# Another order of the products in a feed-forward block, partial sums carried in PSUM by ScalarE, six load places and five split places

## The chip, the cores and the metric

The kernel runs on one core of a Trainium2 chip. The metric is the device time of one execution in microseconds (us). The core has five engines that take part: TensorE (PE) multiplies matrices and writes to PSUM, VectorE (DVE) and ScalarE (ACT) do elementwise work, GpSimd (POOL) does a little arithmetic and issues the accumulating transfers, SyncE (SP) issues all other transfers. Each engine runs its instructions strictly in the order in which the program gives them.

## The reference

Two layers act on x of 256 tokens by 1024 features, in float32. Each layer is a half-step feed-forward network (FFN), a mixer, and a second half-step FFN, each between two RMS norms:

```
def _swiglu(h, wg, wu, wd):
    return (jax.nn.silu(h @ wg) * (h @ wu)) @ wd
...
for l in range(DEPTH):
    f = _swiglu(_rmsnorm(h, ff1_norm_pre[l]), ff1_w_gate[l], ff1_w_up[l], ff1_w_down[l])
    h = h + 0.5 * _rmsnorm(f, ff1_norm_post[l])
    m = _hybrid_mixer(_rmsnorm(h, mix_norm_pre[l]), w_in[l], conv_w[l], conv_b[l], dt_bias[l],
                      a_log[l], d_skip[l], ssd_norm[l], pool_w[l], pool_scale[l], w_out[l])
    h = h + _rmsnorm(m, mix_norm_post[l])
    f = _swiglu(_rmsnorm(h, ff2_norm_pre[l]), ff2_w_gate[l], ff2_w_up[l], ff2_w_down[l])
    h = h + 0.5 * _rmsnorm(f, ff2_norm_post[l])
```

wg and wu are 1024 x 2816, wd is 2816 x 1024. The mixer (state-space heads, pooling, attention) is the same in both kernels. The change concerns the FFNs, of which there are four in a run, and the planner that orders everything.

## The kernel before, in words

**Weights.** Every weight matrix is cut into units of 128 partitions x 2048 float32 (1 MB). A unit is loaded into a `raw` place. Then it is *split* for the multiplication: ScalarE writes `hi`, a copy rounded to the format that TensorE multiplies, and VectorE writes `lo` = raw - hi. A product then takes hi x hi, lo x hi and hi x lo. So each unit costs ScalarE one pass, VectorE one pass and TensorE 12 matmuls of 128x512 (24 for a unit of `wd`, a *down*, which serves both token tiles). There are `RAW_BUFS` = 4 raw places and `SPLIT_BUFS` = 6 places for hi and for lo.

**A block.** Of the 2816 hidden columns of an FFN, columns 512 to 2559 are done in four blocks of 512 (`QUADS`). A block computes the gate and the up projection for both token tiles (0 and 1) by seven products in place of eight (the Strassen-Winograd scheme), on four units: g1, g2 (gate weights, upper and lower half of the features) and u1, u2 (up weights). The products, with the name that the code gives them, the left operand and the weights:

| product | left operand | weights | PSUM bank | how the weights come about |
|---|---|---|---|---|
| g1 | X11 | g1 | pa | loaded |
| T1 | S1 | g1+u1 | pc | VectorE adds u1 into g1's raw place |
| g2 | X12 | g2 | pa, added | loaded |
| u2 | S4 | u2 | pc, added | loaded |
| T2 | S2 | g1+u1+u2 | pb | a DMA issued by GpSimd adds u2 from memory onto the place of g1+u1 |
| T3 | S3 | u1+u2 | pd | a second such DMA adds u2 onto the place of u1 |
| T4 | X22 | g1+u1+u2+g2 | pd, added | VectorE adds g2 into that place |

The two accumulating DMAs can start once T1's sum has read u1 (for T3's weights) and once T1's split has read g1+u1 (for T2's weights). `h0` and `h1` are the results for token tiles 0 and 1; `w2` is a scratch tile. Between the products stand `0` and `1` (the *turns*: TensorE transposes h0 and h1 of the block before, ScalarE and VectorE split them) and `d` (one *down* of the block before: 24 matmuls into the banks `acc`). The list `ORDER` gives the sequence. Bank names in the profile: pa to pd and the turns' banks are `wk` (four places); the turned and split hidden values are `t`; the left operands X are in `xT`, the left operands S in `n`.

**The order.** The program writes its operations to a `Planner`, which sets the order of every engine before anything is emitted: `cost` gives each operation a duration, `arrange` counts latest start times back from TensorE's order (`late`; the allowance for a dependency is `gap` plus a pad), and then runs a list schedule, in which the free places of `raw`, `hi`, `lo` and `wk` count too. It emits the operations in that order (`emit`, line 354 of the kernel before: all instructions of the profile carry that line, so tiles tell them apart). The semaphores that enforce dependencies are put in afterwards, so an estimate in the planner changes only the order. In the code, `Weights` makes loads and splits, `plan_ffn.block` lists the jobs of a block, `product` issues 12 matmuls, `ffn_quad` is the block.

Of the kernel before, what the change touches and what calls it, by code (L numbers as in the profile page):

```python
# [14 lines left out]
AF = mybir.ActivationFunctionType  # L15
# [14 lines left out]
UNIT = 2048  # L30
QDT = 264
PEKEY = 0
PAD = 300.0
TMP, NBUF, ROUNDS = 14, 8, 1
RAW_BUFS = 4
PF, FINE = 2, 'g1 T1 g2'.split()
AHEAD = "".split()
ORDER = "g1 0 T1 1 g2 d T3 T2 d u2 T4".split()
SUMMED = "T3 T2".split()
SPLIT_BUFS = 6  # L40
TAIL = 4

FIRST, QUADS, PAIRS = (0, 1), (2, 4, 6, 8), (10,)
# [95 lines left out]
        return lambda *args, **kw: self.plan.add(self.engine, name, args, kw)  # L139


class Planner:


# [55 lines left out]
    def cost(self, o, views):  # L200
        width = max(v.cols for _, v in views)
        psum = any(v.tile.tag in BANKS for _, v in views)
        e, kind = o.engine, o.name
        o.kind, o.tail = kind, 0.0
        if e == "tensor":
            x = o.args[2] if kind == "matmul" else o.args[1]
            n = x.cols / 2.4
            if kind == "transpose":
                o.busy = 2 * n + 2
            elif x.dtype == F32R:  # L210
                o.busy = n + 14
            elif x.dtype == BF16:
                o.busy = n + 3
            else:
                o.busy = 4 * n + 8
                if x.rows[1] - x.rows[0] <= 64:
                    o.busy /= 2
            o.tail = 205.0
        elif e == "vector":
            o.busy = 1.042 * width + 68 if kind != "memset" else 0.5 * width  # L220
            if kind == "scalar_tensor_tensor":
                o.busy += 0.125 * width
            o.tail = 82.0
        elif e == "scalar":
            func = o.args[2]
            o.busy = 0.844 * width + (60 if psum else 92)
            o.tail = 100.0
            if any(isinstance(v, View) for v in (o.kw.get("scale"), o.kw.get("bias"))):
                o.busy += 90
            if "accum_out" in o.kw:  # L230
                o.busy, o.tail = o.busy + 95, 150.0
            o.kind = {AF.Exp: "exp", AF.Silu: "silu"}.get(func, "any")
        elif o.name == "dma_start":
            x = next(v for _, v in views)
            size = x.cols * 4 * (x.rows[1] - x.rows[0]) / 424.0
            o.kind = "dma"
            o.busy, o.tail = (880.0, size) if e == "gpsimd" else (330.0, size)
        else:
            o.busy, o.tail = 800.0, 0.0

    def gap(self, p, o, why):
        if why == "ORDER":
            return 0.0
        if p.engine == o.engine and p.kind != "dma":
            return p.busy + p.tail + LAG[p.engine, p.engine] if why == "RAW" and p.engine != "tensor" else 0.0
        return p.busy + p.tail + LAG.get((p.engine, o.engine), 55.0)

    def arrange(self, target=None):
        ops = self.ops
        post = [[] for _ in ops]  # L250
        for o in ops:
            for p, why in o.pre.items():
                post[p.n].append((o, self.gap(p, o, why) + (3500.0 + p.tail if p.kind == "dma" else PAD if p.engine != "tensor" else 0)))
        if target is None:
            at, target = 0.0, {}
            for o in ops:
# [7 lines left out]
        ready = [0.0] * len(ops)  # L264
        hand = {e: [o for o in ops if o.engine == e and not o.pre] for e in ENGINES}
        free = dict.fromkeys(ENGINES, 0.0)
        line, idle, table = 0.0, 0.0, "any"
        turn = dict.fromkeys(self.slots, 0)
        places = {k: [(0.0, i) for i in range(n)] for k, n in self.slots.items()}
        for t in self.tiles:  # L270
# [32 lines left out]
        while len(order) < len(ops):  # L303
# [13 lines left out]
                busy += 1300.0 * (table not in ("any", o.kind))  # L317
                table = o.kind
            if o.kind == "dma":
                line = max(s + (600 if e == "sync" else 1500), line) + o.tail * (1 if e == "sync" else 1.5)  # L320
                done = line + o.tail * (0 if e == "sync" else 0.5) + 1700.0
            else:
                done = s + busy + o.tail
            if e == "tensor":
# [97 lines left out]
def hybrid_trunk_kernel(ctx: ExitStack, tc: tile.TileContext, a, out: bass.AP):  # L422
# [200 lines left out]
    def plan_ffn(l, n):  # L623
# [11 lines left out]
        def block(i, src, before):  # L635
# [14 lines left out]
            for s in steps:  # L650
                if s == "d":
                    jobs.append((s, None, None, None))
                    continue
                if s == "g1":
                    k, y = "g1", None
                elif s in ("g2", "u2"):
                    k, y = s, None
                elif s == "T3":
                    k, y = "u1+u2" if "T3" in AHEAD else "u1", None
                elif s == "T1" and "T1" in AHEAD:  # L660
                    k, y = "g1+u1", None
                else:
                    k = "g1+u1" if "T1" in AHEAD else "g1"
                    y = chain[s]
                jobs.append((s, k, y if s not in SUMMED else None, y if s in SUMMED else None))
# [96 lines left out]
    def ffn_quad(i, p, left, turn, downs):  # L762


        tiles = {}
        downs = list(downs)
        for s in ORDER:
            if s in "01":
                turn(int(s))
            elif s == "d":  # L770
                if downs:
                    downs.pop(0)()
            elif s == "g1":
                pa = bank()
                product(pa, left["X11"], p[s, i], True)
                w2 = buf()
                nc.scalar.activation(w2, pa, AF.Copy)
            elif s == "T1":
                pc = bank()
                product(pc, left["S1"], p[s, i], True)  # L780
                h1 = buf()
                nc.scalar.activation(h1, pc, AF.Copy)
            elif s == "T2":
                pb = bank()
                product(pb, left["S2"], p[s, i], True)
                nc.vector.tensor_tensor(w2, pb, w2, op=ALU.add)
                nc.vector.tensor_tensor(pc, pc, w2, op=ALU.subtract)
                tiles["T2"] = 1
                if "T3" in tiles:
                    nc.vector.tensor_tensor(pd, pd, w2, op=ALU.add)  # L790
                    nc.vector.tensor_tensor(h1, h1, pd, op=ALU.subtract)
            elif s == "T3":
                pd = bank()
                product(pd, left["S3"], p[s, i], True)
                tiles["T3"] = 1
                if "T2" in tiles:
                    nc.vector.tensor_tensor(pd, pd, w2, op=ALU.add)
                    nc.vector.tensor_tensor(h1, h1, pd, op=ALU.subtract)
            elif s == "g2":
                product(pa, left["X12"], p[s, i], False)  # L800
                h0 = buf()
                nc.scalar.activation(h0, pa, AF.Silu)
            elif s == "T4":
                product(pd, left["X22"], p[s, i], False)
                nc.scalar.activation(w2, pd, AF.Silu)
                nc.vector.tensor_tensor(h1, h1, w2, op=ALU.mult)
            elif s == "u2":
                product(pc, left["S4"], p[s, i], False)
                nc.vector.tensor_tensor(h0, pc, h0, op=ALU.mult)
        assert not downs  # L810
        return [h0, h1]

# [594 lines left out]
```

## Time and profile before

| | us |
|---|---|
| median of 3 runs | 960.19 |
| lowest and highest | 953.47, 962.56 |
| the profiled execution, its own time | 959.03 |
| its span, first to last instruction | 957.2 |

| engine | busy us | share | instructions |
|---|---|---|---|
| TensorE, matmuls | 924.6 | 97% | 4666 |
| VectorE | 806.0 | 84% | 915 |
| ScalarE | 589.0 | 62% | 799 |
| GpSimd | 54.0 | 6% | 67 |

The granted TensorE clock of the execution is 0.993. The run is, in order: first FFN, mixer, second FFN of layer 0, then the same of layer 1. Busy time of TensorE in the profile is the union of its matmuls' spans, and their ends are modelled, so a stretch that is 100% busy need not be one in which it works at its full rate. Columns of the timeline views: start, time taken, engine, line, operation, output<-inputs, count, and in brackets the idle time before it and what ended that.

### The profile page before, as it was taken

To read this page: it belongs to the slowest core of one execution; us is meant where nothing else is said; L and a number is where in the kernel's file an instruction comes from. 1 tells how busy PE (TensorE), PEld (TensorE's weight loads), DVE (VectorE), ACT (ScalarE), POOL (GpSimd) and SP (SyncE) were. 2 spreads that over 40 slices of the span, in tenths; PEclk is the share of its full clock that TensorE was granted. 3 is DMA by queue.
4 is the path that set the end of the run, shared out by engine and by line. 5 is a ranking of instruction groups with operands and counts; after the bars stand their busy time and mean duration, and the time that the engine had idled before them with its cause. 6 is when DMAs were issued, how large, how long until landed. Compare 5 with 4: busy or idle time off the path is not lost.

```text
span 957.2 us, 12144 instructions
## 1 busy us (share of the span) xinstructions
PE 924.6 (97%) x4666; PEld 768.8 (80%) x4666; DVE 806.0 (84%) x915; ACT 589.0 (62%) x799; POOL 54.0 (6%) x67
## 2 busy tenths in 40 slices
PE   8999999999999999998999999899999999999997
PEld 5878777989988887777988887688998888887796
DVE  6898898889879889888699898886898799889862
ACT  7656656678647746655577565656694576646641
POOL 0000000010002000000020000000000010000000
PEclk9999999999999999999999999999999999999999
DMA  8968877955434887887568787884743277797821
GB/s 340 284 224 261 246 228 265 346 201 196 157 126 127 231 257 243 250 255 290 193 173 294 194 256 271 226 315 157 253 151 132 91 194 264 220 274 240 276 89 45
DMA packets 30878, 211.46 MB, mean 221 GB/s; under 512 B 3426, under 2 KB 3682, under 8 KB 6244
## 3 DMA queue, kind: packets, MB, share of 16 engines
q1 hardware_dynamic: 26212, 177.13, 49.4%
q0 software_dynamic: 4608, 33.56, 18.4%
q8 instruction: 37, 0.61, 0.2%
q14 instruction: 21, 0.17, 0.1%
HBM read 209.62 MB, written 1.05 MB: 220 GB/s over the span
## 4 chain that ended last, share of the span: by engine, by line
PE 32%; DVE 15%; DMA 11%; ACT 5%; issue 5%; DVEq 0%; POOLq 0%; POOL 0%; ACTq 0%
PE wk L354 22%; DMA raw<-in_ff_q 11%; PE acc L354 10%; DVE lo L354 10%; ACT hi L354 5%; DVE raw L354 4%; DVE t L354 1%; DMA raw<-in_ff_d 1%; ACT t L354 0%; DVE h L354 0%; DVEq L1403 0%; DVE n L354 0%; POOLq L1403 0%; POOL s L354 0%; ACTq L354 0%
## 5 line engine op out<-in xcount | busy, mean ns | idle before, releaser
L354 DVE TENSOR_TENSOR lo<-raw,hi 128x2048 fp32r<-128x2048 f32 (+3 forms) x300 | 482.6, 1632 | 78.5 <-ACT hi L354 76.9
L354 ACT ACTIVATE hi<-raw 128x2048 fp32r<-128x2048 f32 (+3 forms) x300 | 406.5, 1386 | 226.6 <-DVE raw L354 91.1
L354 PE MATMUL acc<-hi,t 128*128 128x512 f32 x832 | 217.3, 392 | 1.2 <-DVE t L354 1.0
L354 PE MATMUL wk<-hi,xT 128*128 128x512 f32 (+1 forms) x832 | 213.1, 387 | 5.2 <-DVE t L354 2.9
L354 PEld LDWEIGHTS acc<-hi,t 128*128 128x128 f32 x832 | 154.8, 188 | 35.0 <-DVE t L354 3.2
L354 PEld LDWEIGHTS wk<-hi,xT 128*128 128x128 f32 x832 | 149.6, 188 | 39.1 <-issue 5.6
L354 PE MATMUL wk<-hi,n 128*128 128x512 f32 x512 | 142.7, 406 | 14.1 <-DVE t L354 7.1
L354 PEld LDWEIGHTS wk<-hi,n 128*128 128x128 f32 x512 | 96.4, 193 | 39.6 <-issue 11.9
L354 PE MATMUL acc<-lo,t 128*128 128x512 f32 x416 | 114.2, 390 | 0.0
L354 ACT ACTIVATE t<-wk 128x512 f32<-128x512 f32 (+2 forms) x194 | 85.5, 480 | 41.6 <-PE wk L354 32.3
L354 PE MATMUL wk<-lo,xT 128*128 128x512 f32 (+1 forms) x416 | 108.3, 383 | 1.5 <-DVE lo L354 1.5
L354 PEld LDWEIGHTS acc<-lo,t 128*128 128x128 f32 x416 | 78.1, 188 | 16.5
L354 PEld LDWEIGHTS wk<-lo,xT 128*128 128x128 f32 x416 | 76.2, 188 | 18.0 <-DVE lo L354 2.7
L354 DVE TENSOR_TENSOR t<-wk,t 128x256 fp32r<-128x256 f32 (+1 forms) x140 | 71.0, 517 | 14.5 <-ACT t L354 14.3
L354 PE MATMUL wk<-xT,hi 128*128 128x256 f32 x576 | 77.1, 284 | 0.0
L354 PE MATMUL wk<-lo,n 128*128 128x512 f32 x256 | 72.7, 407 | 1.9 <-DVE lo L354 1.9
L354 PEld LDWEIGHTS wk<-xT,hi 128*128 128x128 f32 x576 | 72.6, 191 | 1.6 <-issue 0.7
L354 DVE TENSOR_TENSOR raw<-raw,raw 128x2048 f32<-128x2048 f32 (+1 forms) x36 | 73.5, 2049 | 0.3
L354 PEld LDWEIGHTS wk<-lo,n 128*128 128x128 f32 x256 | 49.0, 193 | 15.1 <-DVE lo L354 3.2
L354 POOL TENSOR_TENSOR s<-s,halfexp 128x1 f32<-128x1 f32 x28 | 25.3, 902 | 479.3 <-ACT s L354 337.6
L354 POOL DMA_DIRECT2D raw<-in_ff_q x32 | 28.1, 879 | 418.8 <-DVE t L354 268.5
L354 DVE TENSOR_TENSOR n<-acc,gains 128x512 f32<-128x512 f32 x24 | 16.5, 690 | 34.9 <-ACT n L354 34.9
(91 smaller groups left out, 562.1 us busy)
## 6 DMA issues: line engine op xcount, KB each, us to landing
raw<-in_ff_q SPq DMA_DIRECT2D x64, 1024.0 KB, 5.4
raw<-in_ff_d SPq DMA_DIRECT2D x44, 1024.0 KB, 6.5
raw<-in_ff_q POOLq DMA_DIRECT2D x32, 1024.0 KB, 9.0
raw<-in_ff_f SPq DMA_DIRECT2D x16, 1024.0 KB, 4.8
raw<-in_w_in SPq DMA_DIRECT2D x10, 1024.0 KB, 4.8
raw<-in_w_kvz SPq DMA_DIRECT2D x8, 1024.0 KB, 5.3
raw<-in_w_out SPq DMA_DIRECT2D x8, 1024.0 KB, 4.8
gains<-in_gains SPq DMA_DIRECT2D x11, 512.0 KB, 6.5
```

The source lines that it names most:

```text
L354: getattr(getattr(nc, o.engine), o.name)(*map(put, o.args), **{k: put(v) for k, v in o.kw.items()})
```

## The change

1. `ORDER`, the sequence of a block, goes from `g1 0 T1 1 g2 d T3 T2 d u2 T4` to `g1 0 T1 g2 1 d u2 T2 d T3 T4`.
2. The partial sums of the Winograd scheme are carried otherwise. Before, T2 and T3 go into empty banks and VectorE adds the earlier sums afterwards (`w2 = pb + w2`, `pc -= w2`, `pd += w2`, `h1 -= pd`). Now ScalarE copies g1's product from bank pa to bank pb, T2 is multiplied onto it, ScalarE copies pb to bank pd (and to w2), and T3 and T4 are multiplied onto that. VectorE keeps `pc -= w2`, `h1 -= pd`, `h0 = pc*h0` and `h1 *= w2`. Per block VectorE loses two operations of 128x512 and ScalarE gains two.
3. `RAW_BUFS` 4 to 6, `SPLIT_BUFS` 6 to 5; the memory taken is the same (4 + 2x6 and 6 + 2x5 tiles of one size).
4. The planner's idea of a transfer: a new class `Loads` keeps the two DMA queues apart and lets them share when they overlap; sizes are divided by 355 (SP) and 210 (GpSimd) in place of 424, and the allowances before a transfer's user change from 3500 + tail to 2500 (SP) or `MORE` = 6000 (GpSimd).

No matmul, no load and no split is added or taken away; GpSimd's sequence of operations is the same.

```diff
-PAD = 300.0
+PAD, MORE, LATE = 300.0, 6000.0, 2000.0
-RAW_BUFS = 4
+RAW_BUFS = 6
-ORDER = "g1 0 T1 1 g2 d T3 T2 d u2 T4".split()
+ORDER = "g1 0 T1 g2 1 d u2 T2 d T3 T4".split()
-SPLIT_BUFS = 6
+SPLIT_BUFS = 5
...
+class Loads:
+    def __init__(self):
+        self.end, self.spans, self.share = [0.0, 0.0], [[], []], (0.32, 0.68)
+
+    def add(self, which, t, work):
+        t = start = max(t, self.end[which])
+        part = self.share[which]
+        for a, b in self.spans[1 - which]:
+            if b <= t:
+                continue
+            alone = max(a - t, 0.0)
+            if work <= alone:
+                break
+            work -= alone
+            t += alone
+            if work <= (b - t) * part:
+                t, work = t + work / part, 0.0
+                break
+            work -= (b - t) * part
+            t = b
+        t += work
...
-            size = x.cols * 4 * (x.rows[1] - x.rows[0]) / 424.0
+            size = x.cols * 4 * (x.rows[1] - x.rows[0])
-            o.busy, o.tail = (880.0, size) if e == "gpsimd" else (330.0, size)
+            o.busy, o.tail = (880.0, size / 210.0) if e == "gpsimd" else (330.0, size / 355.0)
...
+        if p.kind == "dma":
+            return p.tail + (MORE if p.engine == "gpsimd" else 2500.0)
...
-                line = max(s + (600 if e == "sync" else 1500), line) + o.tail * (1 if e == "sync" else 1.5)
-                done = line + o.tail * (0 if e == "sync" else 0.5) + 1700.0
+                done = loads.add(1, s + 2800, o.tail) + LATE if e == "gpsimd" else loads.add(0, s + 1500, o.tail) + 1500
...
             elif s == "g1":
                 pa = bank()
                 product(pa, left["X11"], p[s, i], True)
-                w2 = buf()
-                nc.scalar.activation(w2, pa, AF.Copy)
...
             elif s == "T2":
-                pb = bank()
-                product(pb, left["S2"], p[s, i], True)
-                nc.vector.tensor_tensor(w2, pb, w2, op=ALU.add)
-                nc.vector.tensor_tensor(pc, pc, w2, op=ALU.subtract)
-                if "T3" in tiles:
-                    nc.vector.tensor_tensor(pd, pd, w2, op=ALU.add)
-                    nc.vector.tensor_tensor(h1, h1, pd, op=ALU.subtract)
+                product(pb, left["S2"], p[s, i], False)
+                pd = bank()
+                nc.scalar.activation(pd, pb, AF.Copy)
+                w2 = buf()
+                nc.scalar.activation(w2, pb, AF.Copy)
+                nc.vector.tensor_tensor(pc, pc, w2, op=ALU.subtract)
+                if done:
+                    nc.vector.tensor_tensor(h0, pc, h0, op=ALU.mult)
             elif s == "T3":
-                pd = bank()
-                product(pd, left["S3"], p[s, i], True)
+                product(pd, left["S3"], p[s, i], False)
+                nc.vector.tensor_tensor(h1, h1, pd, op=ALU.subtract)
+            elif s == "g2":
+                pb = bank()
+                nc.scalar.activation(pb, pa, AF.Copy)
                 product(pa, left["X12"], p[s, i], False)
...
             elif s == "u2":
                 product(pc, left["S4"], p[s, i], False)
-                nc.vector.tensor_tensor(h0, pc, h0, op=ALU.mult)
+                done = True
```

How the instructions move, at two places of the second FFN of layer 0. The numbers behind names are the buffers'.

VectorE before, from T2's split in the third block to the next block's T1: in turn the splits (lo) of T2 and of a down, two pieces of turns (t<-wk), T4's sum, a piece of u2's split, T4, g1 of the next block, T1's sum, then w2 = pb + w2 and pc -= w2. The next two rows, not shown, are pd += w2 and T1's split.

```order
L354 TENSOR_TENSOR lo_3404<-raw_3222,hi_3388 128x2048
L354 TENSOR_TENSOR lo_3422<-raw_3362,hi_3409 128x2048
L354 TENSOR_TENSOR t_3394<-wk_3406,t_3383 128x2x128
L354 TENSOR_TENSOR t_3441<-wk_3373,t_3402 128x2x128
L354 TENSOR_TENSOR raw_3222<-raw_3222,raw_3254 128x2048
L354 TENSOR_TENSOR lo_3459<-raw_3390,hi_3428 128x2048
L354 TENSOR_TENSOR t_3441<-wk_3406,t_3402 128x2x128
L354 TENSOR_TENSOR lo_3482<-raw_3222,hi_3462 128x2048
L354 TENSOR_TENSOR lo_3495<-raw_3438,hi_3476 128x2048
L354 TENSOR_TENSOR raw_3438<-raw_3438,raw_3464 128x2048
L354 TENSOR_TENSOR t_3376<-wk_3491,t_3376 128x512
L354 TENSOR_TENSOR wk_3380<-wk_3380,t_3376 128x512
```

VectorE now, from T2's split in the same block to the next block's T1: splits of T2 and a down, T4's sum, splits of T3, T4 and the next g1, T1's sum, pc -= w2, h1 -= pd, h0 = pc*h0, T1's split.

```order
L383 TENSOR_TENSOR lo_3452<-raw_3151,hi_3439 128x2048
L383 TENSOR_TENSOR lo_3465<-raw_3298,hi_3449 128x2048
L383 TENSOR_TENSOR raw_3151<-raw_3151,raw_3246 128x2048
L383 TENSOR_TENSOR lo_3490<-raw_3183,hi_3461 128x2048
L383 TENSOR_TENSOR lo_3507<-raw_3151,hi_3492 128x2048
L383 TENSOR_TENSOR lo_3525<-raw_3392,hi_3504 128x2048
L383 TENSOR_TENSOR raw_3392<-raw_3392,raw_3418 128x2048
L383 TENSOR_TENSOR wk_3378<-wk_3378,t_3522 128x512
L383 TENSOR_TENSOR t_3415<-t_3415,wk_3518 128x512
L383 TENSOR_TENSOR t_3425<-wk_3378,t_3425 128x512
L383 TENSOR_TENSOR lo_3568<-raw_3392,hi_3551 128x2048
```

T3 takes the place of u2 in this stretch; the turns have moved out of it, ahead of T2; three operations of 128x512 stand ahead of T1's split as before, though other ones.

TensorE before, after the second down of that block: u2 onto pc (wk_3380), T4 onto pd (wk_3471), then the next block's g1 (wk_3578).

```order
L354 MATMUL wk_3380<-hi_3428,n_2899 128x512 x4
L354 MATMUL wk_3380<-lo_3459,n_2899 128x512 x4
L354 MATMUL wk_3380<-hi_3428,n_3020 128x512 x4
L354 MATMUL wk_3471<-hi_3462,xT_137 128x512 x4
L354 MATMUL wk_3471<-lo_3482,xT_137 128x512 x4
L354 MATMUL wk_3471<-hi_3462,xT_160 128x512 x4
```

TensorE now, after the second down: T3 onto pd (wk_3518), five matmuls of the next g1 (wk_3555), T4 onto pd, the rest of g1.

```order
L383 MATMUL wk_3518<-hi_3461,n_2882 128x512 x4
L383 MATMUL wk_3518<-lo_3490,n_2882 128x512 x4
L383 MATMUL wk_3518<-hi_3461,n_2893 128x512 x4
L383 MATMUL wk_3555<-hi_3504,xT_140 128x512 x4
L383 MATMUL wk_3555<-lo_3525,xT_140 128x512
L383 MATMUL wk_3518<-hi_3492,xT_140 128x512 x4
L383 MATMUL wk_3518<-lo_3507,xT_140 128x512 x4
L383 MATMUL wk_3518<-hi_3492,xT_162 128x512 x4
L383 MATMUL wk_3555<-lo_3525,xT_140 128x512 x3
L383 MATMUL wk_3555<-hi_3504,xT_162 128x512 x4
```

u2, which adds onto a bank that VectorE has just changed, has moved ahead of T2; between T3 and T4, which share a bank that VectorE reads in between, stand five matmuls of the next block.

More of the change, by code (lines that the diff above doesn't have):

```diff
@@ L139, in __getattr__ @@
         return lambda *args, **kw: self.plan.add(self.engine, name, args, kw)
+class Loads:
[18 more added lines that the diff above has]
+        t += work
+        self.end[which] = t
+        self.spans[which].append((start, t))
+        return t
 class Planner:
@@ L252, in arrange @@
             for p, why in o.pre.items():
-                post[p.n].append((o, self.gap(p, o, why) + (3500.0 + p.tail if p.kind == "dma" else PAD if p.engine != "tensor" else 0)))
+                post[p.n].append((o, self.gap(p, o, why) + (PAD if p.engine != "tensor" else 0)))
         if target is None:
@@ L266, in arrange @@
         free = dict.fromkeys(ENGINES, 0.0)
-        line, idle, table = 0.0, 0.0, "any"
+        loads, idle, table = Loads(), 0.0, "any"
         turn = dict.fromkeys(self.slots, 0)
@@ L658, in block @@
                 elif s == "T3":
-                    k, y = "u1+u2" if "T3" in AHEAD else "u1", None
+                    k, y = "u1", None if "T3" in SUMMED else "u2"
                 elif s == "T1" and "T1" in AHEAD:
@@ L762, in ffn_quad @@
     def ffn_quad(i, p, left, turn, downs):
-        tiles = {}
         downs = list(downs)
+        pa = pb = pc = pd = h0 = h1 = done = None
         for s in ORDER:
@@ L783, in ffn_quad @@
             elif s == "T2":
-                pb = bank()
-                product(pb, left["S2"], p[s, i], True)
-                nc.vector.tensor_tensor(w2, pb, w2, op=ALU.add)
-                nc.vector.tensor_tensor(pc, pc, w2, op=ALU.subtract)
-                tiles["T2"] = 1
-                if "T3" in tiles:
-                    nc.vector.tensor_tensor(pd, pd, w2, op=ALU.add)
-                    nc.vector.tensor_tensor(h1, h1, pd, op=ALU.subtract)
-            elif s == "T3":
-                pd = bank()
-                product(pd, left["S3"], p[s, i], True)
[L795 to L799, printed above, removed]
+                product(pb, left["S2"], p[s, i], False)
[6 more added lines that the diff above has]
+                    nc.vector.tensor_tensor(h0, pc, h0, op=ALU.mult)
+            elif s == "T3":
+                product(pd, left["S3"], p[s, i], False)
+                nc.vector.tensor_tensor(h1, h1, pd, op=ALU.subtract)
+            elif s == "g2":
+                pb = bank()
+                nc.scalar.activation(pb, pa, AF.Copy)
                 product(pa, left["X12"], p[s, i], False)
@@ L808, in ffn_quad @@
                 product(pc, left["S4"], p[s, i], False)
-                nc.vector.tensor_tensor(h0, pc, h0, op=ALU.mult)
+                done = True
+                if pd is not None:
+                    nc.vector.tensor_tensor(h0, pc, h0, op=ALU.mult)
         assert not downs
```

## The prediction

> **What bounds the kernel now.** I read the page's busy times first, then stretches of the run, then the chain of waits, then one block instruction by instruction.
>
> ```profile
> PE 924.6 (97%) x4666; PEld 768.8 (80%) x4666; DVE 806.0 (84%) x915; ACT 589.0 (62%) x799; POOL 54.0 (6%) x67
> PE wk L354 22%; DMA raw<-in_ff_q 11%; PE acc L354 10%; DVE lo L354 10%; ACT hi L354 5%; DVE raw L354 4%; DVE t L354 1%; DMA raw<-in_ff_d 1%; ACT t L354 0%; DVE h L354 0%; DVEq L1403 0%; DVE n L354 0%; POOLq L1403 0%; POOL s L354 0%; ACTq L354 0%
> ```
>
> TensorE is busy 97% of the span, and yet a third of the chain lies on transfers and splits (raw<-in_ff_q, lo, hi, raw). Where? The stretches below are the four FFNs up to the end of their blocks and, second row, a mixer; the columns are length, then busy time of PE, PEld, DVE, ACT, POOL, then clock and DMA share.
>
> ```profile
> 10.00:168.00 158.00, 150.07 (x659) 118.59 (x660) 137.50 (x120) 101.74 (x108) 8.16 (x9) 1.00 0.82 263
> 168.00:309.00 141.00, 140.96 (x877) 125.14 (x876) 121.83 (x218) 94.12 (x191) 10.03 (x11) 1.00 0.53 192
> 309.00:437.00 128.00, 122.67 (x546) 98.40 (x544) 112.76 (x86) 78.35 (x72) 6.08 (x7) 1.00 0.81 242
> 495.00:624.00 129.00, 124.68 (x557) 100.33 (x556) 116.15 (x89) 81.30 (x74) 6.12 (x7) 1.00 0.82 247
> 791.00:906.00 115.00, 111.00 (x496) 89.44 (x495) 102.98 (x74) 70.90 (x62) 5.24 (x6) 1.00 0.80 253
> ```
>
> In the mixer TensorE never rests (140.96 of 141.00). It idles in the FFNs: 7.93 + 5.33 + 4.32 + 4.00 = 21.6 us. Two blocks of the second FFN of layer 0, each measured from the end of T1's split to the next:
>
> ```profile
> 348.12:382.22 34.10, 32.54 (x145) 26.06 (x143) 29.61 (x22) 19.93 (x18) 1.75 (x3) 1.00 0.80 246
> 382.22:416.15 33.93, 32.08 (x140) 25.29 (x140) 29.60 (x22) 19.82 (x18) 1.72 (x2) 1.00 0.81 249
> ```
>
> How long would TensorE need alone? A fed stretch gives the rate; the last row gives four transposes:
>
> ```profile
> 384.48 1.98 PE L354 MATMUL wk<-hi,xT 128*128 128x512 f32 x8
> 386.30 1.07 PE L354 MATMUL wk<-lo,xT 128*128 128x512 f32 x4
> 387.21 1.07 PE L354 MATMUL wk<-hi,xT 128*128 128x512 f32 x4
> 388.12 0.60 PE L354 MATMUL wk<-ident,t 128*128 128x128 f32 x4
> 388.47 1.17 PE L354 MATMUL wk<-hi,n 128*128 128x512 f32 x4
> ```
>
> From 384.48 to 387.21 there are 12 matmuls, 0.227 us each; four transposes take 0.35. A block has 7 x 12 + 2 x 24 = 132 matmuls and 8 transposes: 132 x 0.227 + 0.7 = 30.7 us. So a block of 33.93 wastes 3.2 us of TensorE, only 1.85 of which shows as idle; the rest is in "busy" time that runs below the rate. DVE is busy 29.6: not full either. The chain says what holds the block:
>
> ```profile
> 381.82 0.40 issue
> 382.22 10.52 DMA raw<-in_ff_q
> 392.82 1.80 ACT hi L354
> ...
> 413.45 2.30 DVE lo L354
> 415.75 0.40 issue
> ```
>
> It is a loop with one turn per block. T1's split ends, GpSimd issues T2's accumulating transfer, this lands 10.5 us later, T2 is split, and DVE then works without a break until the next T1's split. DVE's own rows of that turn, where its two waits for the accumulating transfers stand in brackets:
>
> ```profile
> 388.28 2.29 DVE L354 TENSOR_TENSOR lo<-raw,hi 128x2048 fp32r<-128x2048 f32 x1 [0.87 <-ACT hi L354]
> 394.77 4.49 DVE L354 TENSOR_TENSOR lo<-raw,hi 128x2048 fp32r<-128x2048 f32 x2 [3.26 <-ACT hi L354]
> 399.18 0.75 DVE L354 TENSOR_TENSOR t<-wk,t 128x256 fp32r<-128x256 f32 x2
> 399.84 2.28 DVE L354 TENSOR_TENSOR raw<-raw,raw 128x2048 f32<-128x2048 f32 x1
> 402.04 2.28 DVE L354 TENSOR_TENSOR lo<-raw,hi 128x2048 fp32r<-128x2048 f32 x1
> 404.25 0.42 DVE L354 TENSOR_TENSOR t<-wk,t 128x256 fp32r<-128x256 f32 x1
> 404.58 4.48 DVE L354 TENSOR_TENSOR lo<-raw,hi 128x2048 fp32r<-128x2048 f32 x2
> 409.10 2.29 DVE L354 TENSOR_TENSOR raw<-raw,raw 128x2048 f32<-128x2048 f32 x1
> 411.31 0.68 DVE L354 TENSOR_TENSOR t<-wk,t 128x512 f32<-128x512 f32 x1
> 412.02 1.30 DVE L354 TENSOR_TENSOR wk<-wk,t 128x512 f32<-128x512 f32 x2
> 413.45 2.29 DVE L354 TENSOR_TENSOR lo<-raw,hi 128x2048 fp32r<-128x2048 f32 x1
> ```
>
> The loop, by starts of rows: 381.82 to 392.82 is 11.0 for issue and landing; to 394.77, 1.95 for ScalarE's hi; to 415.75, 20.98 of DVE. Sum 33.93.
>
> **The change, part by part.**
>
> *Other order in a block.* In the new order DVE works in the loop on the splits of T2, a down, T3, T4, the next g1 and T1, on two sums, and on three operations of 128x512. That is the old content with T3 in u2's place, the same pass of 128x2048. What has left it are the turns: 399.18 to 399.84 and 404.25 to 404.58, 0.66 + 0.33 = 0.99 us. They now stand before T2's split, under the wait for the transfer, as does u2's split. The first part, g2 to the last turn, is 3 splits of 2.2 and 0.68 + 4 x 0.37, 8.8 us, still shorter than 11.0 + 1.95; so the wait remains and is what ends last. New turn: 11.0 + 1.95 + 19.99 = 32.94 us, against TensorE's 30.7. I count four such turns per FFN (three from T1 to T1, the last from T1 to T4's split), 16 in all: 16 x 0.99 = -15.8 us.
>
> *Sums carried in PSUM.* DVE loses w2 = pb + w2 and pd += w2, 2 x 0.69 a block. I take nothing for it: h1 -= pd and h0 = pc*h0 take their places in the loop, and outside it DVE waits anyway (0.87 + 3.26 above). ScalarE gains two copies a block. A copy from PSUM to PSUM isn't in the trace; the nearest rows are these:
>
> ```profile
> L354 ACT ACTIVATE t<-wk 128x512 f32<-128x512 f32 x94 | 53.6, 592 | 18.5 <-PE wk L354 18.3
> L354 DVE TENSOR_TENSOR wk<-wk,t 128x512 f32<-128x512 f32 x32 | 20.7, 694 | 0.5
> ```
>
> 0.59 us by ScalarE's own row, 0.69 if writing PSUM costs as on DVE. I take 0.59: 1.2 us a block on an engine that is busy 19.8 of 33.93. pd = copy of pb waits for T2's last matmul, and behind it on ScalarE stand the copy to w2 and the hi of T4 or of the next T1; TensorE's 24 matmuls of a down (5.4 us) cover it before T3 needs pd. If the cover is gone, T3 comes 1.2 us late, inside TensorE's slack of 32.94 - 30.7 = 2.2. I take 0, bounds 0 and +0.5 a block where both fall together.
>
> *Waits of TensorE on DVE.* Before, u2 waits for pc -= w2 and T4 for h1 -= pd, at every block's end and worst at the FFN's:
>
> ```profile
> 412.78 1.20 PE L354 MATMUL wk<-hi,n 128*128 128x512 f32 x4 [0.84 <-DVE wk L354]
> 416.48 1.16 PE L354 MATMUL wk<-hi,xT 128*128 128x512 f32 x4 [0.63 <-DVE t L354]
> 437.91 1.20 PE L354 MATMUL wk<-hi,n 128*128 128x512 f32 x4 [2.49 <-DVE t L354]
> ```
>
> u2 now stands before T2 and waits for nothing new. T4 still waits for h1 -= pd, behind five matmuls of g1 (1.1 us). Inside the blocks such waits are the loop's slack showing up and are already counted. At the FFN's end, 2.49 lies after the loop: between 0 and -2.5 each; I take -1.0, four times, -4.
>
> *Five split places, six load places.* A split place less is one unit less that DVE may be ahead when the blocks begin: 12 x 0.227 = 2.7 us. That ScalarE does meet full places is seen in the waits:
>
> ```profile
> ACT hi L354 <- PE wk L354: 27.5, 14, 4.1
> ```
>
> Per FFN this costs 0 (lead not used up) to +2.7. Since TensorE idles at the end of every FFN, the lead is used up; but it is not always full at the start. I take half, +1.35 x 4 = +5.4. The mixers hold TensorE at 100% and have the same number of instructions: 0, bounds of 3 us either way for the new order there. Two more load places let SP load earlier. Loads already come in time: the waits in brackets above are for accumulating transfers. 0 for that.
>
> *The landing.* T2's transfer took 10.52, of which part is T3's transfer, issued 4.1 us earlier and served first, and part a load:
>
> ```profile
> 378.10 0.87 POOL L354 DMA_DIRECT2D raw<-in_ff_q  x1 [29.10 <-DVE t L354]
> 386.33 1.92 ACT L354 ACTIVATE hi<-raw 128x2048 fp32r<-128x2048 f32 x1 [3.24 <-DMA raw<-in_ff_q]
> q0 software_dynamic: 244, 1.74, 77.1%
> q1 hardware_dynamic: 141, 1.08, 26.1%
> ```
>
> The first lands in 8.2 us; the last two rows (382 to 393) show the accumulations with 77% of the DMA engines and one load of 1.08 MB with 26%. GpSimd's sequence is unchanged, so T3's still goes first though T2 is now wanted first. When does a load fall beside it? Before, SP issues a load 5.6 us after T1's split. Now the next g1's load waits for the down's place, free after about 4.4 us. Nearly the same: I take 10.5, with 8.2 and 13.3 (one more load, below) as bounds.
>
> The Trainium skill speaks against the six places here: "DMA: Bandwidth & Descriptors", section "Queues, rings and completion order", says that each DMA engine goes round-robin between the queues that have work, a packet at a time. By that rule a load that six places let start early takes bandwidth from the transfer that the loop waits for, and the time would be that of the slower rival below rather than that of my sum. The shares above agree with the rule; the trace does not show what six places do.
>
> *Sum.* 959.0 - 15.8 - 4 + 5.4 = 944.6 for the profiled execution, which lies 1.2 below the median of 960.19: 945.8 by the median, say 945.
>
> **The rivals.**
>
> *The landing gets shorter and TensorE becomes the bound.* At a landing of 8.2 the turn is 32.94 - 2.3 = 30.6, TensorE's own time. For it: two unhurried load places could keep loads away from the accumulations. Against: the two accumulations still follow each other by 4 us. What can be won is all of TensorE's waste in the FFNs: 21.6 idle and some 1.5 of slow running in two blocks per FFN, 12, less 5 that belongs to the starts: -29, 930 us. Chance 0.17.
>
> *The lost place eats the gain.* The lead costs its full 2.7 in every FFN and the FFN's ends do not improve: -15.8 + 10.9 = -5, 955 us. For it: the ScalarE waits on full places; against: they are only 27.5 us in 14 pieces, none inside the blocks shown. Chance 0.27.
>
> *Slower: loads beside the accumulation.* With two more places, SP issues one more load within the 11 us after T1's split, as soon as a place is free. The engines have no room while accumulating (77.1 + 26.1%), so a load adds all that it takes from them: 26.1% of 11 us is 2.9 us for 1.08 MB, 2.8 for a unit. The turn becomes 32.94 + 2.8 = 35.7, 1.8 more than before, and 16 x 1.8 = +29: 989 us. It decides once the landing exceeds 10.5 + 1.0 = 11.5. For it: T3's and T2's transfers already share; against: the load places come free at about the same point of the loop as before. Chance 0.11.
>
> *The change doesn't do what it says*, because the planner undoes the order: ruled out, the rows above show T3 behind T2 and the new copies; the planner's new transfer model acts only through these rows.
>
> **How the numbers follow.** Forecast 945 with chance 0.45, own range 936 to 953 (split place and FFN ends at their bounds, 3 us for the mixers); 930 with 0.17; 955 with 0.27; 989 with 0.11. The range leaves out the slower case, 0.11, and the far side of the best one, about 0.07: 928 to 961. One per cent, 9.6 us, is about what a measurement of this kernel can tell from no change: faster means below 950.6, slower above 969.8. Faster: 0.17 and nearly nine tenths of 0.45, 0.57. Slower 0.11. Within 1%: 0.32.
>
> **What would show it.** In the changed kernel's trace: the interval between two ends of T1's split near 32.9 us (30.7: first rival; above 34: the slower one); the chain still turning through raw<-in_ff_q with 10 to 11 us a piece, now with T2 alone waiting and DVE's waits of about 4 us in one piece; about 32 fewer DVE and 32 more ScalarE instructions, PSUM copies of about 0.6 us; TensorE's idle time in the four FFN stretches down from 21.6 to about 12; the 2.49 at the end of the blocks gone or smaller; ScalarE waiting longer on TensorE for places. The prediction is wrong if the landing changes by more than 1 us, if the first block of an FFN, which runs in pieces and not by the steady loop, shifts by more than a turn's gain, or if the mixers change by more than 3 us.

## The result and the profile after

The changed kernel took 933.26 us (median; 931.55 to 934.31) beside 961.38 for the kernel before on the same chip (953.47 to 963.58): a ratio of 0.971 with an interval of 0.9655 to 0.9766. The profiled execution's span is 932.6 us against 957.2, at a clock of 0.999. I had forecast 945.

The page of the changed kernel, busy times and the chain of waits:

```profile
span 932.6 us, 12101 instructions
PE 917.6 (98%) x4666; PEld 766.9 (82%) x4666; DVE 788.1 (85%) x883; ACT 603.7 (65%) x831; POOL 52.5 (6%) x67
PE 75%; DVE 9%; issue 5%; ACT 5%; DMA 5%; DVEq 0%; POOLq 0%; POOL 0%; SPq 0%; ACTq 0%
```

TensorE was a third of the chain and is now three quarters of it. The 32 fewer DVE and 32 more ScalarE instructions are there. The stretches of the four FFNs, in the columns of the prediction's table:

```profile
10.00:160.00 150.00, 146.01 (x642) 115.58 (x642) 130.35 (x109) 102.75 (x115) 8.05 (x9) 1.00 0.86 282
305.00:430.00 125.00, 124.99 (x561) 102.22 (x560) 110.75 (x84) 82.92 (x81) 6.99 (x8) 1.00 0.81 242
483.00:604.00 121.00, 120.36 (x538) 97.86 (x538) 104.74 (x81) 80.32 (x79) 7.02 (x8) 1.00 0.83 246
760.00:880.00 120.00, 119.32 (x533) 97.02 (x534) 103.72 (x81) 79.54 (x79) 7.00 (x8) 1.00 0.82 243
```

TensorE's idle time there is 3.99 + 0.01 + 0.64 + 0.68 = 5.3 us, against 21.6 before; the stretches hold nearly the same work, 2274 matmuls here and 2258 there. Over the whole execution TensorE's idle time fell from 957.2 - 924.6 = 32.6 us to 932.6 - 917.6 = 15.0, which is 17.6 of the 24.6 us by which the span shrank. The other 7.0 are "busy" time that ran below the rate, as a fed block shows. Below is the chain of the changed kernel over two blocks of the second FFN (start, length, what, instructions):

```profile
342.03 14.73 PE wk L383 x68
356.76 5.49 PE acc L383 x24
362.25 5.61 PE wk L383 x24
367.86 5.47 PE acc L383 x24
373.33 14.73 PE wk L383 x68
```

No transfer and no split is in it. One block of 140 instructions takes 373.33 - 342.03 = 31.30 us, and that is TensorE's own pace; before, the same 140 showed 32.08 busy within 33.93. Of the transfers, only these pieces of 10 us or more are still in the whole chain, against seven before:

```profile
32.92 17.45 DMA raw<-in_ff_q
522.99 11.83 DMA raw<-in_ff_q
799.96 12.59 DMA raw<-in_ff_q
```

### The profile page after: what moved, and what is told of

It is laid out like the page before. It is cut to its first block, busy times and chain, and to the rows that moved or that the text cites. A ratio compares the mean times of both kernels' runs of the same rounds, so it can differ in the third digit from the quotient of the medians.

```text
span 932.6 us, 12101 instructions
## 1 busy us (share of the span) xinstructions
PE 917.6 (98%) x4666; PEld 766.9 (82%) x4666; DVE 788.1 (85%) x883; ACT 603.7 (65%) x831; POOL 52.5 (6%) x67
## 4 chain that ended last, share of the span: by engine, by line
PE 75%; DVE 9%; issue 5%; ACT 5%; DMA 5%; DVEq 0%; POOLq 0%; POOL 0%; SPq 0%; ACTq 0%
PE wk L383 48%; PE acc L383 26%; DVE lo L383 6%; DMA raw<-in_ff_q 4%; ACT hi L383 4%; DVE raw L383 2%; DVE t L383 1%; DMA raw<-in_ff_f 1%; ACT t L383 1%; ACT n L383 0%; DVE xT L383 0%; DVE n L383 0%; ACT xT L383 0%; ACT wk L383 0%; ACT L383 0%
## 5 line engine op out<-in xcount | busy, mean ns | idle before, releaser
L383 PE MATMUL acc<-hi,t 128*128 128x512 f32 x832 | 221.3, 394 | 1.1 <-ACT t L383 0.6
L383 ACT ACTIVATE t<-wk 128x512 f32<-128x512 f32 (+2 forms) x194 | 88.5, 484 | 93.3 <-PE wk L383 54.2
L383 PE MATMUL wk<-hi,n 128*128 128x512 f32 x512 | 139.5, 398 | 1.1 <-ACT wk L383 1.1
L383 PEld LDWEIGHTS wk<-lo,xT 128*128 128x128 f32 x416 | 76.2, 188 | 15.8 <-DVE lo L383 0.3
L383 DVE TENSOR_TENSOR t<-wk,t 128x256 fp32r<-128x256 f32 (+1 forms) x124 | 60.1, 498 | 26.5 <-ACT t L383 25.9
L383 PE MATMUL wk<-lo,n 128*128 128x512 f32 x256 | 70.4, 397 | 0.1
L383 DVE TENSOR_TENSOR n<-acc,gains 128x512 f32<-128x512 f32 x24 | 16.6, 691 | 34.5 <-ACT n L383 34.3
```

Of the source, the lines that this page charges most:

```text
L383: getattr(getattr(nc, o.engine), o.name)(*map(put, o.args), **{k: put(v) for k, v in o.kw.items()})
```

## Experiments

Unless said otherwise, the ratio is to the kernel before, run beside it, whose median lay between 960.07 and 961.38. Differences between two variants are differences of medians that were mostly not taken beside each other, so 1 or 2 us of them mean nothing.

**1. The accumulating transfers left out.** Both kernels without the 32 transfers that GpSimd issues. This leaves out the addition of u2 into T2's and T3's weights, and nothing else.

```diff
-        for v, src in add:
-            nc.gpsimd.dma_start(self.raw[v][:, :cols], src, accum_op=ALU.add)
+        for v, src in ():
+            pass
```

> The kernel before without the 32 accumulating transfers: the weights of T2 and T3 lack u2, everything else is done as before. If the loop through T2's transfer holds the blocks (33.9 us a turn of which 11.0 for issue and landing), TensorE becomes the bound and the time falls to 925 to 935 us. If TensorE waits for VectorE's sums or for the splits whatever the transfer does, it stays above 950.

> The changed kernel without the 32 accumulating transfers (the weights of T2 and T3 lack u2). If the changed kernel is no longer held by the loop in most blocks, 926 to 933 us, nearly the same as the kernel before without them; if the loop still holds it, 915 to 925 us.

Before without them: 928.49, ratio 0.9681 (0.9638 to 0.9724). Changed without them: 931.87, 0.9714 (0.9671 to 0.9758). The old kernel loses 32 us to these transfers, the changed one 933.26 - 931.87 = 1.4, less than its scatter. So waiting on them was what the old kernel could win, and nearly all of it has been won. In the old kernel without them VectorE still makes the sums behind the next T1's sum, as before, and yet TensorE's T1 products come 31.2 us apart from the second FFN on. Late sums alone do not stop TensorE. Since the planner orders anew for each kernel, these figures are no exact floor (experiment 6 goes below 931.87).

**2. The order with the old sums, and the old order in a like arrangement.** First the changed kernel with VectorE making the sums as before:

```diff
...
-                pd = bank()
-                nc.scalar.activation(pd, pb, AF.Copy)
-                w2 = buf()
-                nc.scalar.activation(w2, pb, AF.Copy)
+                nc.vector.tensor_tensor(w2, pb, w2, op=ALU.add)
...
-                product(pd, left["S3"], p[s, i], False)
+                pd = bank()
+                product(pd, left["S3"], p[s, i], True)
+                nc.vector.tensor_tensor(pd, pd, w2, op=ALU.add)
```

> The changed kernel with the sums by VectorE as before (w2 = pb + w2, pd += w2; T2 and T3 into empty banks), in the new order, with the new places and planner. If the sums in PSUM matter (VectorE loses 2 x 0.69 us a block, and T4 waits for one operation of VectorE less), 940 to 950 us. If VectorE waits anyway, as the prediction has it, within 4 us of 933.

931.08, ratio 0.9705 (0.9667 to 0.9743). Carrying the sums in PSUM brings nothing here: 2.2 us less without it (with T2's transfer first, experiment 6, it is 3.0 us better with it). Either is small beside what a measurement of this kernel can tell. Then the changed kernel with a sequence nearer the old one, sums still in PSUM:

```diff
-ORDER = "g1 0 T1 g2 1 d u2 T2 d T3 T4".split()
+ORDER = "g1 0 T1 1 g2 d T2 T3 d u2 T4".split()
```

> The changed kernel with the products of a block back in the old places as far as the new sums allow it: g1, turn 0, T1, turn 1, g2, down, T2, T3, down, u2, T4 (T2 must stand ahead of T3, since its bank is copied). Sums by ScalarE, places and planner as in the changed kernel. If the gain is the order (the turns and u2 moved under the wait for T2's accumulating transfer), most of it goes: 950 to 960 us, and the turn from T1 to T1 is back at 33.5 to 35 us. If it is the sums in PSUM or the places and the planner, the time stays within 5 us of 933.

971.42, ratio 1.0113 (1.007 to 1.0155). The output of this arrangement isn't the network's, so only its time is read. Every instruction is there; that a sum which ScalarE copies into a bank gets lost there is a guess that no run tested. This sequence costs 38 us against the new one, with the issues of T2's transfer 35.7 us apart (mean of the twelve intervals within the FFNs). It isn't the old order, so it doesn't price that; experiment 5 does.

**3. The places.** The changed kernel with the old numbers, and the old one with the new numbers, together and singly.

```diff
-RAW_BUFS = 6
-SPLIT_BUFS = 5
+RAW_BUFS = 4
+SPLIT_BUFS = 6
```

> The changed kernel with four load places and six split places. If the two more load places carry the gain, 945 to 960 us and T2's landing in an FFN's first block back at 11 to 13 us. If, as the prediction has it, the split place lost costs up to 2.7 us per FFN and the load places give nothing, 925 to 933 us.

1042.85, ratio 1.087 (1.0812 to 1.0928): 110 us more than the changed kernel. In a window of the second FFN (385 to 425 us) two pieces of that kernel's chain start where SyncE issues a load; the chain's pieces, then SyncE's rows:

```profile
384.03 6.78 DMA raw<-in_ff_q
390.83 3.73 ACT hi L383 x2
...
422.54 7.53 DMA raw<-in_ff_q
```

```profile
384.03 0.33 SPq L383 DMA_DIRECT2D raw<-in_ff_q  x1
...
422.54 0.33 SPq L383 DMA_DIRECT2D raw<-in_ff_q  x1
```

With four places the loads themselves are late, and the path runs through them. TensorE stalls in a second way as well, for 3 us in this block, where the hi that it needs stands behind the PSUM copies on ScalarE (in the chain the copies start at 399.63 and the hi at 400.72):

```profile
402.57 1.65 PE L383 MATMUL acc<-hi,t 128*128 128x512 f32 x3 [3.03 <-ACT hi L383]
```

So the new order needs the new numbers of places. That it is the load places is read from this chain; the two numbers weren't varied singly here. How much of the 110 us is the loads' and how much that second stall's wasn't separated.

The old kernel with six and five, and with five split places and four load places:

```diff
-RAW_BUFS = 4
+RAW_BUFS = 6
-SPLIT_BUFS = 6
+SPLIT_BUFS = 5
```

> The kernel before with six load places and five split places, nothing else. The prediction: 0 for the load places, 0 to +2.7 us per FFN for the split place, so 960 to 972 us. If the places carry the gain: 935 to 950 us.

```diff
-SPLIT_BUFS = 6
+SPLIT_BUFS = 5
```

> Before with five split places in place of six, nothing else. My prediction took +5.4 us for it (bounds 0 and +10.9: up to 2.7 in each FFN): 965.8. A second theory, from the places-alone run that was 6.7 faster: the place costs nothing, 960, and all of the 6.7 is the load places'. A third: it costs 5 and the load places bring 12.

953.72, ratio 0.9952 (0.9919 to 0.9986), and 954.89, ratio 0.9941 (0.9907 to 0.9975). The two don't differ. So the load places are worth nothing on the old order, and one split place less costs nothing; it seems even to gain some 5 us, the wrong sign for my +5.4. The trace of the second shows where a gain could come from. With five split places the planner sets VectorE's sums (407.39 and 408.11) ahead of the next T1's sum (412.11), where before they stood behind it (411.31 and 412.02 behind 409.10 in the rows of the prediction):

```profile
407.39 0.68 DVE L354 TENSOR_TENSOR t<-wk,t 128x512 f32<-128x512 f32 x1
408.11 1.29 DVE L354 TENSOR_TENSOR wk<-wk,t 128x512 f32<-128x512 f32 x2
412.11 2.28 DVE L354 TENSOR_TENSOR raw<-raw,raw 128x2048 f32<-128x2048 f32 x1
```

From the first T1 to the last, TensorE needs 94.4 us there in the second FFN, against 98.8 before. But this profiled execution, one of the slower ones of its kernel (958.61), has the old span, 956.8: what it saves in the blocks it loses at the FFNs' ends, where one product waits 3.13 us for VectorE's sums (at 442.59; 2.49 before) and another 3.17 (at 910.87).

**4. The planner's transfer model.** It changes only the order in which things stand. The changed kernel with the old model (the old `gap`, allowances and `line` in place of `Loads`), and the old kernel with the new model:

```diff
-        if p.kind == "dma":
-            return p.tail + (MORE if p.engine == "gpsimd" else 2500.0)
...
-                done = loads.add(1, s + 2800, o.tail) + LATE if e == "gpsimd" else loads.add(0, s + 1500, o.tail) + 1500
+                line = max(s + (600 if e == "sync" else 1500), line) + o.tail * (1 if e == "sync" else 1.5)
+                done = line + o.tail * (0 if e == "sync" else 0.5) + 1700.0
```

> The changed kernel with the planner's old idea of transfers (no overlap of the two queues, old allowances). If the late loads in the plan carry a part, 938 to 955 us with other engine orders at the starts of the FFNs. If the new order of the block carries all, within 4 us of 933.

971.24, ratio 1.0114 (1.0066 to 1.0162): without the model the new order is 11 us slower than the old kernel. The waits of TensorE in that kernel (total us, times, longest), where the turns that ScalarE copies come late:

```profile
PE wk L354 <- ACT t L354: 18.0, 7, 3.4
```

> The kernel before with the planner's new idea of transfers, nothing else. The prediction took nothing for it: within 5 us of 961. If the late loads in the plan matter by themselves: below 952 us.

941.48, ratio 0.9821 (0.9771 to 0.9871). The model alone brings 19 us, more than half of all. What does it move? VectorE's sequence at the end of the third block of the second FFN, shortened: what it is for, then the tile that it writes; a turn's piece between u2 and T4 is left out. Before:

```
T4's sum      raw
u2            lo
T4            lo
next g1       lo
next T1's sum raw
w2 = pb + w2  t
pc -= w2      wk
pd += w2      wk
next T1       lo
```

and in the kernel with the new model:

```
T4's sum      raw
u2            lo
w2 = pb + w2  t
T4            lo
pc -= w2      wk
pd += w2      wk
next g1       lo
next T1's sum raw
...
next T1       lo
```

The sums have moved ahead of the next g1 and the next T1's sum, and w2 = pb + w2 ahead of T4's split too. TensorE's u2 and T4 wait for them. The same stretch in the trace of that kernel, VectorE's rows and then TensorE's u2 and T4:

```profile
404.74 0.68 DVE L383 TENSOR_TENSOR t<-wk,t 128x512 f32<-128x512 f32 x1
405.34 2.28 DVE L383 TENSOR_TENSOR lo<-raw,hi 128x2048 fp32r<-128x2048 f32 x1
407.54 1.29 DVE L383 TENSOR_TENSOR wk<-wk,t 128x512 f32<-128x512 f32 x2
408.74 2.28 DVE L383 TENSOR_TENSOR lo<-raw,hi 128x2048 fp32r<-128x2048 f32 x1
411.06 2.29 DVE L383 TENSOR_TENSOR raw<-raw,raw 128x2048 f32<-128x2048 f32 x1
```

```profile
409.79 1.10 PE L383 MATMUL wk<-hi,n 128*128 128x512 f32 x4
410.73 1.09 PE L383 MATMUL wk<-lo,n 128*128 128x512 f32 x4
411.66 1.10 PE L383 MATMUL wk<-hi,n 128*128 128x512 f32 x4
412.60 1.08 PE L383 MATMUL wk<-hi,xT 128*128 128x512 f32 x4
```

u2 starts at 409.79 without a wait, 2.2 us after the sums begin (407.54). Before, at 412.78 and 416.48, both products had waited. And the loop of the accumulating transfer? It did not get shorter: the mean of twelve intervals from one issue of T2's transfer to the next within an FFN is 34.8 us before and 35.4 here. What differs is how far TensorE lags behind the splits. Here are GpSimd's issue of T2's transfer, which follows T1's split at once, and TensorE's T1 (its lo matmuls), in blocks 2 and 4 of the second FFN. Before:

```profile
348.12 0.88 POOL L354 DMA_DIRECT2D raw<-in_ff_q  x1 [3.26 <-DVE lo L354]
416.15 0.87 POOL L354 DMA_DIRECT2D raw<-in_ff_q  x1 [3.26 <-DVE lo L354]
```

```profile
355.85 1.10 PE L354 MATMUL wk<-lo,n 128*128 128x512 f32 x4
423.38 1.10 PE L354 MATMUL wk<-lo,n 128*128 128x512 f32 x4
```

With the new model:

```profile
349.14 0.88 POOL L383 DMA_DIRECT2D raw<-in_ff_q  x1 [3.25 <-DVE lo L383]
418.12 0.87 POOL L383 DMA_DIRECT2D raw<-in_ff_q  x1 [3.26 <-DVE lo L383]
```

```profile
356.99 1.10 PE L383 MATMUL wk<-lo,n 128*128 128x512 f32 x4
419.42 1.10 PE L383 MATMUL wk<-lo,n 128*128 128x512 f32 x4
```

Before, the split units stand 355.85 - 348.12 = 7.7 us ahead of TensorE in the second block and still 423.38 - 416.15 = 7.2 in the fourth: a lead of which 7.2 us are never spent, because TensorE stops at u2 and T4 instead. With the sums moved forward it is 7.9 and then 1.3: TensorE runs at (419.42 - 356.99) / 2 = 31.2 us a block while VectorE takes (418.12 - 349.14) / 2 = 34.5, and lives on the lead until the blocks are over. The other two FFNs behind the first show the same: in their fourth blocks the lead is 7.2 us before and 1.0 with the new model.

This accounts for part of the 19.9 us by which this execution's span (937.3) is shorter. From the first T1 of an FFN to its last, TensorE saves 10.3 us in the three later FFNs and loses 1.4 in the first; up to the first T1 it loses 1.8. The remaining 12.8 us lie between an FFN's last T1 and the next FFN's first, or the end. Part of that is the wait of 2.49 us at the second FFN's end, which is gone, but the model moves other things there too, and these weren't varied singly. Nor was the place of the sums: that it frees the blocks is read from these traces and from the same move in experiment 3.

**5. What the order adds.** Before with the new model and the new places, the old order and sums.

```diff
-RAW_BUFS = 4
-SPLIT_BUFS = 6
+RAW_BUFS = 6
+SPLIT_BUFS = 5
... (and the planner's new model, as in experiment 4)
```

> Before, with the new transfer model of the planner and with six load and five split places; the order of the block and VectorE's sums are the old ones. It is the arm that is still missing: the changed kernel without its order. First theory (model and places carry the gain and the order adds little): the model alone gave 941.5, the places alone took 6.7 off, so 935 to 937, at most 4 us above the changed kernel's 933.3. Second theory (the order is what uses them): the places bring nothing once the model is there, 940 to 943, so that 7 to 9 us of the gain are the order's; the interval from one end of T1's split to the next then stays at 34 us or more, against 31.9 in the changed kernel.

941.02 (936.91 to 941.49), ratio 0.9781 (0.9746 to 0.9816). The second theory holds: the places add nothing to the model (941.48), and the order adds 941.02 - 933.26 = 7.8 us, or 9.9 with VectorE's sums (931.08). The mean interval between T2's issues is 34.5 us here, 33.5 in the changed kernel (the 31.9 of the expectation is that of single turns).

**6. T2's transfer first.** The changed kernel, with GpSimd issuing T2's accumulating transfer ahead of T3's; then the same with VectorE's sums.

```diff
-        for v, src in add:
-            nc.gpsimd.dma_start(self.raw[v][:, :cols], src, accum_op=ALU.add)
+        adds = [nc.gpsimd.dma_start(self.raw[v][:, :cols], src, accum_op=ALU.add) for v, src in add]
+        for x, y in zip(adds, adds[1:]):
+            y.pre[x] = "ORDER"
```

> The changed kernel with the two accumulating transfers of a block issued the other way round: T2's first, T3's behind it. If the ten microseconds of T2's landing come from sharing with T3's, T2's lands in about 8 and T3's in about 10. What that is worth: without any accumulating transfers the changed kernel took 931.9, so at most 1.5 us, 931.5 to 933.5. A rival: T3's transfer now waits behind T1's split, is issued about 4 us later and its weights come too late for T3, 2 to 3 us per block, 965 to 980.

> The changed kernel with both edits that cost or bring nothing apart: VectorE makes the sums (931.1 against 933.3 with the sums in PSUM), and T2's accumulating transfer goes first. By the reading that TensorE is the bound and 16 PSUM copies only load ScalarE: 929 to 932, the best of all with the whole computation. Rival: the two are within the scatter of the changed kernel, 932 to 935; if T3's weights are late, 960 or more.

927.9 (927.17 to 929.25), ratio 0.9657 (0.9624 to 0.9689), 5.4 us below the changed kernel, no run of either reaching into the other's range, and the best of all kernels here, with the whole computation; 930.91, ratio 0.9688 (0.9654 to 0.9721), with VectorE's sums. The first gains more than the 1.5 us that I allowed. GpSimd issues both transfers at 373.19 in the third block; ScalarE's rows then, T2's hi first:

```profile
382.53 1.92 ACT L383 ACTIVATE hi<-raw 128x2048 fp32r<-128x2048 f32 x1
388.52 1.92 ACT L383 ACTIVATE hi<-raw 128x2048 fp32r<-128x2048 f32 x1 [1.24 <-DMA raw<-in_ff_q]
```

T2's weights were there when ScalarE came to them, at most 382.53 - 373.19 = 9.3 us after the issue; T3's, second now, 15.3 us after it, and they held up neither VectorE nor TensorE. The page's chain of that kernel:

```profile
PE 96%; ACT 2%; issue 1%; DMA 1%; DVE 0%; DVEq 0%; POOLq 0%; POOL 0%; SPq 0%
```

No accumulating transfer is left in it. Most of the gain lies in the first FFN, where TensorE's idle time falls from 3.99 to 1.60 us:

```profile
10.00:160.00 150.00, 148.40 (x669) 119.92 (x669) 134.98 (x112) 105.29 (x115) 8.16 (x9) 1.00 0.89 296
```

From its first to its last issue of T2's transfer, that FFN takes 99.2 us against 104.3; the transfer of 17.45 us in the changed kernel's chain is gone. The rest of the path is TensorE's own.

## Why the prediction was right, and where it wasn't

*The direction and the bound.* Right: before was held in the FFNs by what hangs on the accumulating transfers (32 us, experiment 1), and what can be won is TensorE's waste there. My 29 us for all of it was near.

*The turn.* The mean interval between T2's issues went from 34.8 to 33.5 us, 1.26 a turn against my 0.99. That the two figures lie close is luck. Nearly all of the change is in the first interval of the three later FFNs, 36.4 to 38.0 us before and 31.9 to 32.1 after: there T2's transfer is issued 7.2 us behind T3's instead of 3 to 4, and lands in 7.9 to 8.1 us instead of 10.7 to 13.6. In the first FFN that interval grew from 35.9 to 39.7. The steady turns behind it, of which my sum spoke, take 33.75 us in the mean before and 33.63 after in the later FFNs. So one of the signs that I had named for being wrong did come, a first block that shifts by more than a turn's gain; the mixers stayed within their 3 us (1.8 us shorter each).

And the loop's interval isn't the gain. **The step that failed is "new turn times 16"**, with its companion that the waits at u2 and T4 "are the loop's slack showing up and are already counted". That takes a block of TensorE to be one turn of the loop. The kernel with the model alone has turns of 35.4 us, longer than before, and is 19 us faster. An FFN has only four blocks. In the FFNs after the first the splits are 14 us ahead of TensorE in the first block and 7.7 to 9.1 in the second (old kernel), and this lead pays for an excess of some 3 us a turn, if nothing inside the block stops TensorE. In the old kernel the late sums did. So those waits were a cost, and not only the loop's shadow. It takes both: without the transfers the late sums stop nothing (experiment 1). In the first FFN the lead is only 0.2 us at the second block of the old kernel; there the three turns took 104 us before and after.

*The FFN's end.* Between the last T1 of an FFN and the norm behind it the four FFNs took 14.4 us less in all. I had booked 4 for the ends and 4 x 0.99 for the last turns. From T1 to T1 TensorE saved 11.8, what 12 x 0.99 gives, but not in my way: five of the twelve blocks ran at 31.2 to 31.4 us before and gained nothing, one of the others gained nothing either, and the remaining six gained 1.9 to 2.8 us each.

*The planner's model.* I took 0, because it "acts only through these rows", and put the rows down to `ORDER`. In fact the model alone moves the sums and the turns on the old order too: -19 us alone, and the new order without it is 11 us slower than the old kernel. This is the term that was mis-sized. The order, which I had priced at -15.8, brought 8 to 10 us once model and places were there (experiment 5).

*TensorE's own time.* 31.30 us a block, not 30.7: the 0.227 us came from matmuls with xT; the 24 of `wk` at 362.25 take 0.234 each.

*Sums in PSUM.* Right: 0 in the sum, and 931.08 without them. The copy was bounded by 0.59 and 0.69 us; it took 0.585:

```profile
L383 ACT ACTIVATE wk<-wk 128x512 f32<-128x512 f32 x32 | 18.7, 585 | 24.1 <-PE wk L383 24.0
```

*Waits of TensorE on DVE.* The 2.49 at the FFN's end is gone, as are nearly all of them. TensorE's waits on VectorE's sums and splits before, and all that is left of them:

```profile
PE wk L354 <- DVE t L354: 9.9, 8, 2.5
PE wk L354 <- DVE wk L354: 6.7, 6, 1.6
PE wk L354 <- DVE lo L354: 3.4, 5, 0.9
```

```profile
PE wk L383 <- DVE t L383: 1.7, 5, 0.6
```

That is 20.0 us down to 1.7 (and 0.5 before `acc`). What remains on VectorE beside it is the wait for the left operands `n`, 2.3 us, 2.9 before. I had booked 4.

*Places.* Wrong in both halves, with little effect on the sum: the split place costs nothing measurable (I took +5.4; both old kernels with five came out lower), and the load places, "0 for that", are worth nothing on the old order, while the two numbers together are worth 110 us on the new one. I had looked for waits on loads in the old order only.

*The landing.* Right for blocks 2 to 4 in the mean: 10.5 taken as unchanged; T2's transfer landed in 9.98 us before and 10.22 after. The first blocks moved by more, 3 to 6 us down in the later FFNs and 7.4 up in the first.

*The rivals.* The first one named 930 and TensorE as the bound, which is what came, but by a shorter landing in every turn, which did not; experiment 6 shows that this road is there too, for 5 us more. The slower rival came in three transfers and not in the loop: the second blocks of the last two FFNs took 11.83 and 12.59 us (9.8 and 9.3 before), and the first T2 transfer of the run 17.45, against 10.0 before. In this last one plain loads moved 3.23 MB beside it, with 44.6% of the DMA engines, where before they had moved 0.64 MB (queue, packets, MB, share; before, then after):

```profile
q1 hardware_dynamic: 78, 0.64, 15.4%
q1 hardware_dynamic: 442, 3.23, 44.6%
```

For the other two it was 27% and 33%, after 16% and 11% before. So the longer landings are those with more loads beside them; that the loads are the cause wasn't tested by a run. The rule of the Trainium skill, "DMA: Bandwidth & Descriptors", section "Queues, rings and completion order", is that each DMA engine goes round-robin between the queues that have work. These shares agree with it. "The lost place eats the gain" fell with experiment 3.

So 945 was 12 us too high, and the result lies 3 us below the forecast case's own range: the right engine became free, by another route than the turn I had shortened. That 945 came so near is luck as well: 15.8 us were booked for a shorter steady turn that did not come, and nothing for the model, which brought 19.

## What to carry to other kernels

Before multiplying a loop's saving by its number of turns, measure the lead of the engine that feeds over the one that is fed, at the first and the last turn: if it stays, the stall is somewhere inside the turn, and if it shrinks, the loop is being paid from stock. In a kernel whose order a planner makes, a change of its cost model is a change of the order and has to be built alone before it is booked at nothing. Order, places and model here are one edit: the new order without the new model gave 1.011, without its places 1.087, and the model alone 0.982.

## What the hardware showed unexpectedly

- Two accumulating transfers of 1 MB issued back to back: the first had landed within 9.3 us, the second 15.3 us after the first's issue. With the second issued 5 us behind the first (374.49 and 379.47 of the changed kernel), they landed after 8.1 and 9.2 us; issued 7.2 us behind (305.79 and 312.99), after 7.9 and 8.1.
- A ScalarE copy of 128x512 from PSUM to PSUM takes 0.585 us, one to an SBUF tile 0.593 (`t<-wk`, 94 of them in the same kernel): no difference worth having.
- The stalling kernel with four load places shows a granted clock of 0.964, the fed ones 0.998 and 0.999. Which is cause and which effect, no run tells.
